# RWKV's low-rank products made for all tokens ahead of the S5 mixer instead of inside each RWKV step

## The chip, the cores and the metric

The kernel runs on one core of a Trainium2 chip. The metric is the time of one execution on the device in microseconds (us). The engines are TensorE (PE for products, PEld for weight loads), VectorE (DVE), ScalarE (ACT), GpSimd (POOL) and SyncE (SP), which here only issues DMAs. L909 means line 909 of the kernel; the lines of the kernel before and of the changed one differ, and the text says which is meant.

## The reference

One layer of a decoder step for 1024 prompt tokens and 8 single sample tokens (1032 columns), model width 1024: half-step SwiGLU FFN, then two token mixers side by side (S5, a diagonal complex state space, and RWKV-7) merged by gates, then a second FFN. What matters here are the three low-rank products of the RWKV branch, two of rank 64 (`rwkv_w2` for the decay, `rwkv_a2` for the key rate) and one of rank 128 (`rwkv_g2` for the output gate), each to 512 channels:

```python
def _wkv7_step(s, inp):                      # one token of the RWKV state, per head
    r, dec, k, v, a, b = inp
    sa = jnp.einsum('bhij,bhj->bhi', s, a)
    s = s * dec[:, :, None, :] + sa[..., None] * b[:, :, None, :] + v[..., None] * k[:, :, None, :]
    return s, jnp.einsum('bhij,bhj->bhi', s, r)

# _rwkv_branch: wd, ad (64 columns each) and gd (128) are parts of the mixed projection
w = -jax.nn.softplus(-(p['rwkv_w0'] + jnp.tanh(wd) @ p['rwkv_w2'])) - 0.5
decay = jnp.exp(-jnp.exp(w))
a = jax.nn.sigmoid(p['rwkv_a0'] + ad @ p['rwkv_a2'])
g = jax.nn.sigmoid(gd) @ p['rwkv_g2']
...
o = (yn + bonus) * g

# _layer
h = h + 0.5 * gt1 * _swiglu(n, p['ffn1_w1'], p['ffn1_w3'], p['ffn1_w2'])
proj = u @ p['w_in']                         # S5 input, RWKV's r k v wd ad gd, two sets of gates
mixed = cur + p['mu_shift'] * (prev - cur)   # token shift
y_s5, ... = _s5_branch(s5_in, ...);  y_rwkv, wkv1 = _rwkv_branch(mixed, ...)
m = jax.nn.sigmoid(gates[..., :D_MODEL]) * y_s5 + jax.nn.sigmoid(gates[..., D_MODEL:]) * y_rwkv
h = h + gt2 * (m @ p['w_out'])               # then a second half-step FFN and a norm
```

All inputs and outputs are fp32.

## The kernel before, in words

Activations lie transposed: 128 channels on the partitions, tokens along the columns, in three chunks of 344 columns (`CH`, slices `cs(c)`). A dense product of fp32 data is made as a split product: weights and activations are each split into a high and a low part of type fp32r (`split`: a cast on ACT, a subtraction on DVE), and high x high (L155), high x low (L156) and low x high (L157) are added in PSUM. The RWKV products inside a step are plain fp32, which PE makes in several passes.

The program's stages, by their time in the profile: FFN 1 (to some 870 us), the input projection, whose RWKV columns are evicted through tiles named "gate" (pool `mp`, four buffers under one tag) and written to DRAM (`sMix`) by SP; the S5 stage (984.9 to 1104.2), which begins with the S5 columns of the projection (`s5_in`, L1427 to L1429) and goes on to `s5_mix`; the RWKV stage (1104.2 to 1548); then the rest of the gate columns, the merge and FFN 2.

In the RWKV stage `rw_run` works through 16 parts of the sequence, each 128 tokens of two of the four channel quarters (`rw_part`). Its loop runs the preparation (`rw_prep`, `rw_solve`) six and four steps ahead of the state chain (`rw_chain`) and of the output (`rw_tail`). In each step `rw_prep` makes the decay and key-rate products of its part (L909: rank 64 padded with zeros to 128 rows, `rw_wa2`) into an "sv" bank and applies the sigmoids on ACT (L912, L914); `rw_tail` makes the gate's product (L1154) and multiplies by it from PSUM (L1155). `rw_sample_vectors` and `rw_sample` do the same for the eight sample tokens, with small products.

Beside the RWKV steps run the gate columns' tiles (`gate_tiles`: L155 to L157, 24 products for each chunk, then a sigmoid eviction to a "gate" tile at L1450, written to DRAM). These are called fillers below: they don't depend on RWKV, and the scheduler puts them into PE's row between the steps' short products. The scheduler sets one order per engine ahead of time, from priorities: a block inside `high_priority(offset=...)` is ordered as though it stood earlier in the program. PSUM banks in the RWKV stage: "mm" 2 (the fillers), "sv" 2, "qd" 2, "ch" 1, "y" 1; in the S5 stage "mm" 4 and "s5" 4. An engine runs its row strictly in order.

Of the kernel before, what the change touches and what calls it, by code (L numbers as in the profile page):

```python
# [65 lines left out]
class Net:  # L66
# [755 lines left out]
    def rw_init(self, rows, keep, tag):  # L822
# [12 lines left out]
        wa2 = self.t(keep, [P, T], "rw_wa2")[:, 0:1024].rearrange("p (z f) -> p z f", z=2)  # L835
        nc.gpsimd.memset(wa2, 0.0)
        nc.sync.dma_start(wa2[0:64, 0, :], i["rwkv_w2"])
        nc.sync.dma_start(wa2[64:128, 1, :], i["rwkv_a2"])
        g2 = self.t(keep, [P, 512], "rw_g2")
        nc.sync.dma_start(g2, i["rwkv_g2"])  # L840
        self.wa2, self.g2w = wa2, g2
# [11 lines left out]
    def rw_lora(self, wad, gd):  # L853

        nc = self.nc
        nc.scalar.activation(wad[0:64, :], wad[0:64, :], AF.Tanh)
        nc.scalar.activation(gd, gd, AF.Sigmoid)
        self.wad, self.sgd = wad, gd
# [35 lines left out]
    def rw_prep(self, n, pool):  # L894
# [11 lines left out]
        pt = self.t(self.pp, [P, 2, 256], "sv")  # L906
        for p, ts in pairs:
            for z in range(2):
                nc.tensor.matmul(pt[:, z, ts], self.wa2[:, z, p * P:(p + 1) * P], self.wad[:, tok], start=True, stop=True)  # L909
        sw, b = new("sw"), new("pb", 2)  # L910
        for p, ts in pairs:
            nc.scalar.activation(sw[:, ts], pt[:, 0, ts], AF.Sigmoid, bias=col("w0", p))  # L912
        for p, ts in pairs:
            nc.scalar.activation(b[:, ts], pt[:, 1, ts], AF.Sigmoid, bias=col("a0", p))  # L914
# [208 lines left out]
    def rw_tail(self, n, py, bon, pool):  # L1123
# [5 lines left out]
        tok, pairs = self.rw_part(n)  # L1129
        s1 = self.t(pool, [P, 4], "t_s1")  # L1130
# [13 lines left out]
        pt, pg = (py[:, z].rearrange("p j t -> p (j t)") for z in (1, 0))  # L1144
# [8 lines left out]
        for p, ts in pairs:  # L1153
            nc.tensor.matmul(pg[:, ts], self.g2w[:, p * P:(p + 1) * P], self.sgd[:, tok], start=True, stop=True)  # L1154
        v.tensor_mul(o, o, pg)  # L1155
# [64 lines left out]
    def rw_sample_vectors(self, pool):  # L1220
# [4 lines left out]
        mx = self.t(pool, [P, 3, 4, NB], "smm")  # L1225
# [4 lines left out]
        for w, dst in enumerate((r, kf, vv)):  # L1230
            for p in range(4):
                nc.sync.dma_start(mx[:, w, p], self.mix_src(p, w, smp))
            v.tensor_copy(dst, mx[:, w].rearrange("p a b -> p b a"))
        yield
        pt = ps([P, 2, 4, NB])
        for p in range(4):
            pc = slice(p * P, (p + 1) * P)
            for z in range(2):
# [540 lines left out]
```

## Time and profile before

| what | value |
|---|---|
| time, median of 3 runs | 2614.97 us (2613.99 to 2616.88) |
| the profiled execution's own time | 2611.84 us |
| its span in the trace | 2610.0 us |
| mean granted PE clock | 0.994 |
| PE busy | 2538.7 us, 97% |
| DVE busy | 1456.4 us, 56% |
| ACT busy | 804.8 us, 31% |
| POOL busy | 330.2 us, 13% |

The shares are averages over stages with different limits; the rows below divide them by stretch. PE's matmuls are pipelined: the duration of one in the trace (0.32 us for 128x344) is longer than the distance between two starts, and the costs below go by starts. A wait is put down to the engine whose signal came last.

### The profile page before, as it was taken

The page shows a single profiled execution, that of the slowest core. Times are in us where ns is not written, and L with a number is a line of the kernel's source. Part 1 is how long each engine was busy: PE and PEld are TensorE (multiplying, and loading weights), DVE is VectorE, ACT ScalarE, POOL GpSimd, SP SyncE. Part 2 cuts the span into 40 slices and gives each one's busy share as a digit, 9 for nine tenths or more (in the row PEclk, how much of TensorE's full clock was granted, in tenths as well). Part 3 has the DMA queues.
Part 4 walks back from the last instruction along what each step waited for, and adds up shares of the span by engine and source line. Part 5 has one row for each costly group of instructions (what it writes and reads, how often), then busy time and mean ns, then how long its engine had stood idle before and what let it go on. Part 6 is the DMA issues. An engine that isn't in the chain of part 4 may idle for free.

```text
span 2610.0 us, 46191 instructions
## 1 busy us (share of the span) xinstructions
PE 2538.7 (97%) x18175; PEld 2390.7 (92%) x18175; DVE 1456.4 (56%) x3716; ACT 804.8 (31%) x1610; POOL 330.2 (13%) x973
## 2 busy tenths in 40 slices
PE   7999999999999999989999999999999999999998
PEld 4899999999999998878877889999999999999997
DVE  5533446555556827687888736476843444444435
ACT  4311111111223422466666543312511111111113
POOL 0000002777100001022232201100000000000001
PEclk9999999999999999999999999999999999999999
DMA  8343332212211414443333337533211111111101
GB/s 273 115 141 116 120 117 75 67 59 72 66 61 46 143 37 132 138 107 78 80 77 83 79 108 229 168 117 103 65 56 42 41 49 49 49 49 49 49 10 66
DMA packets 301677, 233.70 MB, mean 90 GB/s; under 512 B 79954, under 2 KB 265075, under 8 KB 301460
## 3 DMA queue, kind: packets, MB, share of 16 engines
q1 hardware_dynamic: 298642, 224.57, 29.1%
q0 software_dynamic: 1920, 5.27, 0.5%
q8 instruction: 143, 2.34, 0.4%
q10 hardware_dynamic: 898, 0.91, 0.1%
q14 instruction: 74, 0.61, 0.1%
HBM read 186.23 MB, written 44.45 MB: 88 GB/s over the span
## 4 chain that ended last, share of the span: by engine, by line
PE 85%; DVE 8%; issue 2%; ACT 2%; POOL 1%; DMA 1%; SPq 0%; POOLq 0%; DVEq 0%; ACTq 0%
PE mm L155 24%; PE mm L157 24%; PE mm L156 23%; PE ada L217 2%; PE qd L1071 1%; PE sv L982 1%; PE mm L171 1%; PE mm L170 1%; PE mm L169 1%; PE mm L1427 1%; PE mm L1428 1%; PE mm L1429 1%; PE mm L177 1%; PE sv L909 1%; DMA wada<-w_ada 0%
## 5 line engine op out<-in xcount | busy, mean ns | idle before, releaser
L155 PE MATMUL mm<-xa,wh 128*128 128x344 f32 x1944 | 636.0, 328 | 4.6 <-ACT xa L311 3.9
L157 PE MATMUL mm<-xa,wl 128*128 128x344 f32 x1944 | 630.7, 325 | 0.0
L156 PE MATMUL mm<-xb,wh 128*128 128x344 f32 x1776 | 575.2, 324 | 0.3 <-DVE xb L315 0.3
L121 ACT CAST wh<-wr 128x1024 fp32r<-128x1024 f32 x186 | 194.1, 1048 | 724.9 <-PE mm L156 668.2
L339 DVE SCALAR_TENSOR_TENSOR h<-mm,modG,h 128x344 f32<-128x344 f32 (+1 forms) x600 | 338.2, 571 | 131.6 <-PE mm L157 115.1
L156 PE MATMUL mm<-xa,wh 128*128 128x344 f32 x1256 | 402.5, 321 | 1.5 <-DVE xa L122 1.2
L155 PEld LDWEIGHTS mm<-xa,wh 128*128 128x128 f32 x1944 | 367.4, 189 | 32.6 <-issue 16.6
L157 PEld LDWEIGHTS mm<-xa,wl 128*128 128x128 f32 x1944 | 368.2, 189 | 6.0 <-issue 2.5
L122 DVE TENSOR_TENSOR wl<-wr,wh 128x1024 fp32r<-128x1024 f32 x186 | 229.1, 1232 | 226.1 <-ACT wh L121 224.7
L155 PE MATMUL mm<-xb,wh 128*128 128x344 f32 x1088 | 347.8, 320 | 1.4 <-ACT xb L311 1.4
L157 PE MATMUL mm<-xb,wl 128*128 128x344 f32 x1088 | 347.6, 320 | 0.0
L155 PE MATMUL mm<-gh,wh 128*128 128x344 f32 x1056 | 338.7, 322 | 2.4 <-DVE h L339 1.9
L156 PEld LDWEIGHTS mm<-xb,wh 128*128 128x128 f32 x1776 | 335.9, 189 | 4.4 <-issue 1.0
L157 PE MATMUL mm<-gh,wl 128*128 128x344 f32 x1056 | 337.6, 320 | 0.0
L156 PE MATMUL mm<-gl,wh 128*128 128x344 f32 x1056 | 337.4, 320 | 0.0
L361 DVE TENSOR_TENSOR silu<-silu,mm 128x344 f32<-128x344 f32 x132 | 67.6, 512 | 450.7 <-PE mm L157 404.0
L156 PEld LDWEIGHTS mm<-xa,wh 128*128 128x128 f32 x1256 | 236.7, 189 | 2.3 <-DVE xa L122 1.9
L155 PEld LDWEIGHTS mm<-xb,wh 128*128 128x128 f32 x1088 | 204.3, 188 | 2.1 <-ACT xb L311 2.0
L155 PEld LDWEIGHTS mm<-gh,wh 128*128 128x128 f32 x1056 | 198.2, 188 | 8.6 <-DVE h L339 2.8
L157 PEld LDWEIGHTS mm<-xb,wl 128*128 128x128 f32 x1088 | 204.3, 188 | 0.0
L157 PEld LDWEIGHTS mm<-gh,wl 128*128 128x128 f32 x1056 | 198.5, 188 | 0.2
L156 PEld LDWEIGHTS mm<-gl,wh 128*128 128x128 f32 x1056 | 198.5, 188 | 0.1
(528 smaller groups left out, 3268.5 us busy)
## 6 DMA issues: line engine op xcount, KB each, us to landing
wr<-ffn_w SPq DMA_DIRECT2D x132, 512.0 KB
wada<-w_ada SPq DMA_DIRECT2D x144, 256.0 KB
wr<-w_in SPq DMA_DIRECT2D x34, 512.0 KB
sGate<-gate SPq DMA_DIRECT2D x48, 172.0 KB
gate<-sGate SPq DMA_DIRECT2D x48, 172.0 KB
sMix<-gate SPq DMA_DIRECT2D x36, 172.0 KB
sH<-h SPq DMA_DIRECT2D x8, 516.0 KB
h<-sH SPq DMA_DIRECT2D x8, 516.0 KB
```

The costliest lines, as they stand in the source:

```text
L121: nc.scalar.copy(hi, src)
L122: nc.vector.tensor_sub(lo, src, hi.bitcast(F32))
L155: nc.tensor.matmul(pt, wh, xh[:, cols], start=q == 0 and ends[0], stop=False)
L156: nc.tensor.matmul(pt, wh, xl[:, cols], start=False, stop=False)
L157: nc.tensor.matmul(pt, wl, xh[:, cols], start=False, stop=q == last)
L169: nc.tensor.matmul(pt, wh[:, k], xh[k][:, cols], start=k == 0, stop=False)
L170: nc.tensor.matmul(pt, wh[:, k], xl[k][:, cols], start=False, stop=False)
L171: nc.tensor.matmul(pt, wl[:, k], xh[k][:, cols], start=False, stop=k == last)
L177: self.nc.tensor.transpose(out, in_, self.ident[:k, :k])
L217: nc.tensor.matmul(pt[32 * g:32 * g + 32, :], self.cT[:, k, :], wt, start=k == 0, stop=k == KD - 1)
L339: nc.vector.scalar_tensor_tensor(h[d][:, c0:c0 + np_], pt[:, :np_], g[:, d, 0:1], hin[d][:, c0:c0 + np_], op0=ALU.mult, op1=ALU.add)
L361: nc.vector.tensor_mul(s, s, p3)
```

## The change

The three products leave the RWKV steps. In the changed kernel `rw_lora` splits their weights (in one tile, `rw_w`, ranks 64 and 64 on the two halves of the rows and rank 128 in a second block) and, chunk by chunk, the activations `wad` and `gd` into fp32r pairs. A new function `rw_rates`, called after `s5_in` and before `s5_mix`, makes for three chunks and four channel quarters six products on half the rows (L879, decay on the upper and key rate on the lower half, in turn) and three on all rows (L881), each of 344 columns: 108 in all. ACT evicts the three banks, two with a sigmoid (L886) and one with a copy (L888), into "gate" tiles, and SP writes each (L889, 36 DMAs of 172 KB) to new DRAM tensors `sW`, `sA` and `sG`. The RWKV steps read their 128 tokens back: `rw_prep` 64 reads of 64 KB into `sw` (now two buffers) and `pb`, `rw_tail` 32 into `gq`; the sample functions read their columns with 12 small DMAs in place of their small products and sigmoids. Later, a buffer that was called `rw_wa2` is used again as `rw_w`.

```diff
@@ -832,13 +832,11 @@
                    enumerate(("w0", "a0", "kk", "ka", "lnw", "lnb", "rk", "ka1"))}
-        wa2 = self.t(keep, [P, T], "rw_wa2")[:, 0:1024].rearrange("p (z f) -> p z f", z=2)
-        nc.gpsimd.memset(wa2, 0.0)
-        nc.sync.dma_start(wa2[0:64, 0, :], i["rwkv_w2"])
-        nc.sync.dma_start(wa2[64:128, 1, :], i["rwkv_a2"])
-        g2 = self.t(keep, [P, 512], "rw_g2")
-        nc.sync.dma_start(g2, i["rwkv_g2"])
-        self.wa2, self.g2w = wa2, g2
+        wts = self.t(keep, [P, T], "rw_w")[:, 0:1024].rearrange("p (z f) -> p z f", z=2)
+        nc.sync.dma_start(wts[0:64, 0, :], i["rwkv_w2"])
+        nc.sync.dma_start(wts[64:128, 0, :], i["rwkv_a2"])
+        nc.sync.dma_start(wts[:, 1, :], i["rwkv_g2"])
+        self.lw = wts
     def rw_clear(self, pool):
...
@@ -850,12 +848,45 @@
                     nc.sync.dma_start(self.inv_half(x, h), zero)
-    def rw_lora(self, wad, gd):
+    def rw_lora(self, wad, gd, pool):
         nc = self.nc
         nc.scalar.activation(wad[0:64, :], wad[0:64, :], AF.Tanh)
         nc.scalar.activation(gd, gd, AF.Sigmoid)
-        self.wad, self.sgd = wad, gd
+        w = [self.t(pool, [P, 2, 512], f"lw{z}", F32R) for z in range(2)]
+        for z in range(2):
+            self.split(w[0][:, z], w[1][:, z], self.lw[:, z])
+        def part(c):
+            x = [[self.t(pool, [P, CH], f"lx{q}{z}", F32R, bufs=2) for z in range(2)] for q in range(2)]
+            for (hi, lo), src in zip(x, (wad, gd)):
+                self.split(hi, lo, src[:, cs(c)])
+            return x
+        self.lo = w, part
+    def rw_rates(self, pool, offset):
+        nc = self.nc
+        (wh, wl), part = self.lo
+        for c in range(3):
+            (xh, xl), (gh, gl) = part(c)
+            for p in range(4):
+                pc = slice(p * P, (p + 1) * P)
+                pts = [self.t(self.pp, [P, CH], next(self.banks)) for _ in range(3)]
+                for q, (w, x, g) in enumerate(((wh, xh, gh), (wh, xl, gl), (wl, xh, gh))):
+                    for pt, hs in zip(pts, HS):
+                        nc.tensor.matmul(pt, w[hs, 0, pc], x[hs], start=q == 0, stop=q == 2)
+                for q, (w, x, g) in enumerate(((wh, xh, gh), (wh, xl, gl), (wl, xh, gh))):
+                    nc.tensor.matmul(pts[2], w[:, 1, pc], g, start=q == 0, stop=q == 2)
+                with self.tc.high_priority(offset=offset):
+                    for pt, dst, b in zip(pts, (self.sW, self.sA, self.sG), ("w0", "a0", None)):
+                        o = self.t(pool, [P, CH + 1], "gate")[:, 0:CH]
+                        if b:
+                            nc.scalar.activation(o, pt, AF.Sigmoid, bias=self.rv[b][:, p:p + 1])
+                        else:
+                            nc.scalar.copy(o, pt)
+                        nc.sync.dma_start(dst[p][:, cs(c)], o)
     @staticmethod
...
@@ -903,15 +934,11 @@
             nc.sync.dma_start(kf[:, ts], self.mix_src(p, 1, tok))
-        pt = self.t(self.pp, [P, 2, 256], "sv")
+        sw, b = new("sw", 2), new("pb", 2)
         for p, ts in pairs:
-            for z in range(2):
-                nc.tensor.matmul(pt[:, z, ts], self.wa2[:, z, p * P:(p + 1) * P], self.wad[:, tok], start=True, stop=True)
-        sw, b = new("sw"), new("pb", 2)
+            nc.sync.dma_start(sw[:, ts], self.sW[p][:, tok])
         for p, ts in pairs:
-            nc.scalar.activation(sw[:, ts], pt[:, 0, ts], AF.Sigmoid, bias=col("w0", p))
-        for p, ts in pairs:
-            nc.scalar.activation(b[:, ts], pt[:, 1, ts], AF.Sigmoid, bias=col("a0", p))
+            nc.sync.dma_start(b[:, ts], self.sA[p][:, tok])
         Dp = self.t(pool, [P, 4, 65], "Dp", bufs=2)
...
@@ -1127,6 +1154,9 @@
         tok, pairs = self.rw_part(n)
+        g = self.t(pool, [P, 256], "gq")
+        for p, ts in pairs:
+            nc.sync.dma_start(g[:, ts], self.sG[p][:, tok])
         s1 = self.t(pool, [P, 4], "t_s1")
...
@@ -1150,9 +1180,7 @@
         v.tensor_add(o, o, bon)
-        for p, ts in pairs:
-            nc.tensor.matmul(pg[:, ts], self.g2w[:, p * P:(p + 1) * P], self.sgd[:, tok], start=True, stop=True)
-        v.tensor_mul(o, o, pg)
+        v.tensor_mul(o, o, g)
         for p, ts in pairs:
...
@@ -1551,6 +1568,7 @@
         N.sInv = [[N.t(N.dp, [32 * 1040], f"sInv{j}{z}") for z in range(3)] for j in range(4)]
+        N.sW, N.sA, N.sG = ([N.t(N.dp, [P, T], f"s{x}{p}") for p in range(4)] for x in "WAG")
         N.sS = N.t(N.dp, [64, 384], "sS")
...
@@ -1652,9 +1670,10 @@
-                    N.rw_lora(wad, gd)
                     N.rw_init(N.t(mp, [P, CH + 1], "gate")[0:28, 0:P], wl, "mm")
+                    N.rw_lora(wad, gd, N.pool(s5w, "lw"))
                     N.s5_in(xh, xl, X, usT, N.pool(s5w, "s5i"))
+                    N.rw_rates(mp, 30000)
```

PE just after `s5_in`, before: behind the last S5 projection (mm_10079) and a transposition stand the fillers (mm_10920) at once.

```order
L1428 MATMUL mm_10079<-wl_9867,xa_164 128x512
L1429 MATMUL mm_10079<-wh_9866,xb_172 128x512
L177 MATMUL mm_10106<-cf_58,s_us_10104 128x128 x4
L155 MATMUL mm_10920<-xa_157,wh_10915 128x344
L156 MATMUL mm_10920<-xb_165,wh_10915 128x344
```

PE at the same place in the changed kernel; lx are the split activations, lw the split weights, and mm_10139 to mm_10141 the first three banks (decay, key rate, gate).

```order
L1446 MATMUL mm_10098<-wh_9885,xb_184 128x512
L177 MATMUL mm_10125<-cf_58,s_us_10123 128x128 x4
L879 MATMUL mm_10139<-lx_1534_10131,lw_1509_9857 128x344
L879 MATMUL mm_10140<-lx_1534_10131,lw_1509_9857 128x344
L879 MATMUL mm_10139<-lx_1535_10132,lw_1509_9857 128x344
L879 MATMUL mm_10140<-lx_1535_10132,lw_1509_9857 128x344
L879 MATMUL mm_10139<-lx_1534_10131,lw_1510_9858 128x344
L879 MATMUL mm_10140<-lx_1534_10131,lw_1510_9858 128x344
L881 MATMUL mm_10141<-lx_1536_10133,lw_1509_9857 128x344
L881 MATMUL mm_10141<-lx_1537_10134,lw_1509_9857 128x344
L881 MATMUL mm_10141<-lx_1536_10133,lw_1510_9858 128x344
```

The 108 new products stand in one piece between the S5 projection and the next dense tile, with no other product among them; every bank of three has its own eviction and write.

ACT in the middle of the RWKV stage, before: two evictions of fillers (L1450) with eight rows of the steps between them; the widest such distance before is 35 rows.

```order
L1450 ACTIVATE gate_17308<-mm_17283 128x344
L912 ACTIVATE sw_14658<-sv_14653,rw_vec_9835 128x128 x2
L874 ACTIVATE sw_14658<-sw_14658 128x256
L876 ACTIVATE pr_14667<-sw_14658 128x256
L1150 ACTIVATE t_o_14589<-y_14506,rw_vec_9835 128x128 x2
L877 ACTIVATE pt_14666<-pr_14667 128x256
L930 ACTIVATE pt_14685<-kf_14650,rw_vec_9835 128x128 x2
L121 CAST wh_17430<-wr_17429 128x1024
L880 ACTIVATE pt_14666<-pt_14666 128x256
L1450 ACTIVATE gate_17336<-mm_17311 128x344
```

ACT in the changed kernel, the two ends of the place where the evictions (now L1467) stand furthest apart.

```order
L916 ACTIVATE pt_13729<-sw_13721,cf_58 128x256
L1467 ACTIVATE gate_17422<-mm_17397 128x344
L1126 COPY x_2205_13872<-ch_13839 128x128
L916 ACTIVATE pt_13729<-sw_13721,cf_58 128x256
L1130 COPY SUV_13511<-ch_13839 64x2x64
```

```order
L911 ACTIVATE pt_14899<-pt_14899 128x256
L1467 ACT_TABLE_LOAD
L1467 ACTIVATE gate_17450<-mm_17425 128x344
L913 ACTIVATE pt_14899<-pt_14899 128x256
L1467 ACTIVATE gate_17478<-mm_17453 128x344
```

Between gate_17422 and gate_17450 there are 106 rows of RWKV work, among them those of three steps.

PE at the end of the last filler before that place (mm_17453), and where the next one (mm_17487) begins, in the changed kernel.

```order
L156 MATMUL mm_17453<-xb_184,wh_17392 128x344
L157 MATMUL mm_17453<-xa_176,wl_17393 128x344
L1009 MATMUL sv_14278<-R_14261,bk_14265 128x128 x2
L1009 MATMUL sv_14279<-R_14261,bk_14265 128x128 x2
L1009 MATMUL sv_14278<-R_14261,bk_14265 128x128
```

```order
L1129 MATMUL ch_15014<-x_2432_15019,Y_2370_14692 64x64 x4
L959 MATMUL sv_14921<-pt_14918,cf_58 128x256
L1134 MATMUL ch_15014<-SUV_14681,WS_14674 64x64 x4
L155 MATMUL mm_17487<-xa_169,wh_17482 128x344
L156 MATMUL mm_17487<-xb_177,wh_17482 128x344
```

From the one to the other PE's row holds 73 lines (254 products) of RWKV alone; before, the longest such piece is 26 lines (77 products). Counted from one tail's transposition to the next, before has 32 to 66 fillers in each of the 15 distances; the changed kernel has 20, 0 and 3 in three in the middle and 31 to 54 in the others.

## Rows read from the trace of the kernel before

**Rows 1.** The page, parts 1 and 2: span, shares, PE by slice.
```profile
span 2610.0 us, 46191 instructions
PE 2538.7 (97%) x18175; PEld 2390.7 (92%) x18175; DVE 1456.4 (56%) x3716; ACT 804.8 (31%) x1610; POOL 330.2 (13%) x973
...
PE   7999999999999999989999999999999999999998
...
PEclk9999999999999999999999999999999999999999
```
**Rows 2.** The page, part 4: shares of the chain that ended last.
```profile
PE 85%; DVE 8%; issue 2%; ACT 2%; POOL 1%; DMA 1%; SPq 0%; POOLq 0%; DVEq 0%; ACTq 0%
```
**Rows 3.** Busy time by stretch (columns in the first line): dense, S5, RWKV, six steps.
```profile
core 0: us, PE busy (x) PEld busy (x) DVE busy (x) ACT busy (x) POOL busy (x), PEclk, DMA share, GB/s
600.00:840.00 240.00, 240.00 (x1554) 234.44 (x1553) 128.05 (x314) 53.33 (x103) 48.81 (x202) 1.00 0.20 61
984.90:1104.20 119.30, 113.91 (x1061) 105.48 (x1060) 86.94 (x249) 40.96 (x95) 10.89 (x13) 1.00 0.44 132
1104.20:1548.00 443.80, 419.29 (x4577) 356.52 (x4576) 344.82 (x1096) 281.04 (x641) 109.83 (x174) 0.98 0.34 82
1261.30:1396.80 135.50, 129.00 (x1564) 106.70 (x1560) 119.35 (x381) 93.28 (x222) 41.51 (x67) 0.99 0.34 79
```
**Rows 4.** Groups in 1261.3 to 1396.8: line, tiles, count | busy, mean ns | idle before.
```profile
L157 PE MATMUL mm<-xa,wl 128*128 128x344 f32 x81 | 28.2, 348 | 0.0
L155 PE MATMUL mm<-xa,wh 128*128 128x344 f32 x82 | 28.2, 343 | 0.0
L156 PE MATMUL mm<-xb,wh 128*128 128x344 f32 x81 | 27.6, 341 | 0.0
```
**Rows 5.** Timeline of PE around an L909 group: start us, us, instruction.
```profile
1104.22 1.05 PE L909 MATMUL sv<-wad,rw_wa 128*128 128x128 f32 x8
1105.04 0.41 PE L155 MATMUL mm<-xa,wh 128*128 128x344 f32 x1
1105.28 0.32 PE L156 MATMUL mm<-xb,wh 128*128 128x344 f32 x1
1105.44 0.32 PE L157 MATMUL mm<-xa,wl 128*128 128x344 f32 x1
```
**Rows 6.** Timeline of PE around an L1154 group.
```profile
1235.31 0.61 PE L1154 MATMUL y<-gd,rw_g 128*128 128x128 f32 x4
1235.68 0.40 PE L156 MATMUL mm<-xb,wh 128*128 128x344 f32 x1
1235.92 0.32 PE L157 MATMUL mm<-xa,wl 128*128 128x344 f32 x1
```
**Rows 7.** Groups of the whole span: the products removed and a dense tile's eviction.
```profile
L909 PE MATMUL sv<-wad,rw_wa 128*128 128x128 f32 x128 | 19.2, 298 | 3.6 <-DVE W L987 1.9 <-DVE qt L1016 1.6
L1467 ACT ACTIVATE gate<-mm 128x344 f32<-128x344 f32 x24 | 10.9, 458 | 48.3 <-PE mm L157 30.6 <-DVE gate L1472 11.7 <-DVE xa L122 4.1
L1154 PE MATMUL y<-gd,rw_g 128*128 128x128 f32 x64 | 10.3, 284 | 0.0
```
**Rows 8.** Timeline of PE around fp32 products on half the rows (L982).
```profile
1141.14 1.16 PE L982 MATMUL sv<-R,bk 64*128 64x128 f32 x8
1142.23 0.42 PE L157 MATMUL mm<-xa,wl 128*128 128x344 f32 x1
```
**Rows 9.** A 172 KB tile's write: SP's issue, DMA in half-microseconds, landing from POOL's queue.
```profile
990.88 0.32 SPq L1399 DMA_DIRECT2D sMix<-gate  x1
...
990.80:991.30 0.50, 0.50 (x7) 0.41 (x5) 0.24 (x2) 0.00 (x0) 0.00 (x0) 1.00 0.00 0
991.30:991.80 0.50, 0.50 (x7) 0.42 (x6) 0.47 (x4) 0.00 (x0) 0.00 (x0) 1.00 0.14 55
991.80:992.30 0.50, 0.50 (x7) 0.50 (x6) 0.50 (x2) 0.00 (x0) 0.00 (x0) 1.00 0.82 297
...
DMA to landing us min/median/max: 2.3/2.9/5.6
```
**Rows 10.** Busy time and granted clock in two stretches with an idle PE.
```profile
1150.00:1155.00 5.00, 2.78 (x11) 2.74 (x12) 4.92 (x14) 0.00 (x0) 1.36 (x2) 0.74 0.39 92
1125.00:1130.00 5.00, 2.99 (x21) 2.69 (x22) 3.54 (x13) 1.38 (x4) 2.50 (x5) 1.00 0.50 133
```

More of the change, by code (lines that the diff above doesn't have):

```diff
@@ L1143, in rw_tail @@
         v.tensor_mul(y, y, bc(rn))
-        pt, pg = (py[:, z].rearrange("p j t -> p (j t)") for z in (1, 0))
+        pt = py[:, 1].rearrange("p j t -> p (j t)")
         for j in range(4):
@@ L1224, in rw_sample_vectors @@
         sm = self.sm = self.t(pool, [P, 12, NB, 4], "sm")
-        mx = self.t(pool, [P, 3, 4, NB], "smm")
+        mx = self.smx = self.t(pool, [P, 6, 4, NB], "smm")
         nkk, dec, b, kp, r, vv, kf, sw, tmp, e, y, bon = (sm[:, q] for q in range(12))
@@ L1229, in rw_sample_vectors @@
         ps = lambda shape: self.t(self.pp, shape, self.stag)
-        for w, dst in enumerate((r, kf, vv)):
+        for w, dst in enumerate((r, kf, vv, sw, b, None)):
             for p in range(4):
-                nc.sync.dma_start(mx[:, w, p], self.mix_src(p, w, smp))
-            v.tensor_copy(dst, mx[:, w].rearrange("p a b -> p b a"))
+                src = self.mix_src(p, w, smp) if w < 3 else (self.sW, self.sA, self.sG)[w - 3][p][:, smp]
+                nc.sync.dma_start(mx[:, w, p], src)
+            if dst is not None:
+                v.tensor_copy(dst, mx[:, w].rearrange("p a b -> p b a"))
         yield
[L1235 to L1238, printed above, removed]
-                nc.tensor.matmul(pt[:, z, p], self.wa2[:, z, pc], self.wad[:, smp], start=True, stop=True)
-        perm = lambda x: x.rearrange("p a b -> p b a")
-        v.tensor_add(sw, perm(pt[:, 0]), bc("w0"))
-        v.tensor_add(b, perm(pt[:, 1]), bc("a0"))
-        nc.scalar.activation(sw, sw, AF.Sigmoid)
-        nc.scalar.activation(b, b, AF.Sigmoid)
         self.rw_decay(sw, tmp, e, ((-1.0, lambda f, g: v.tensor_mul(dec, f, g)),))
@@ L1344, in rw_sample @@
         v.tensor_add(y, y, bon)
-        pt = ps([P, 4, NB])
-        for p in range(4):
-            nc.tensor.matmul(pt[:, p], self.g2w[:, p * P:(p + 1) * P], self.sgd[:, smp], start=True, stop=True)
         yield
         yt = self.t(pool, [P, 4, NB], "smt", bufs=1)
-        v.tensor_mul(yt, perm(y), pt)
+        v.tensor_mul(yt, perm(y), self.smx[:, 5])
         for p in range(4):
@@ L1730, in hybrid_step @@
                 m3 = N.pool(st, "m3", 5)
-                old = iter(("wad", "gd", "rw_wa2"))
+                old = iter(("wad", "gd", "rw_w"))
                 def mt(d):
```

## The prediction

> **What bounds the kernel now.** I read the page's shares first: TensorE (PE) is busy 2538.7 of 2610.0 us, and its slices are nearly all nines [rows 1]; the chain that ended last is 85% PE and 8% VectorE (DVE) [rows 2]. So a microsecond taken off PE is worth about one, as long as no other engine takes its place. Where that can happen is read by stage. In a dense stretch PE is busy for all of 240.00 us and starts 1554 matmuls: 0.154 us for one 128x344 product of split weights. In the S5 stage, where the new products go, PE is busy 113.91 of 119.30 us. In the RWKV stage it is busy 419.29 of 443.80, and in six of its steps (1261.3 to 1396.8) 129.00 of 135.50 us with DVE at 119.35 and ScalarE (ACT) at 93.28 [rows 3]. There PE is kept busy by products of the gate columns, which fill between the short products of RWKV: 82 + 81 + 81 = 244 of them in the six steps [rows 4], times 0.154 = 37.7 us. Without them a step of 22.6 us holds (129.0 - 37.7) / 6 = 15.2 us of PE work and 119.35 / 6 = 19.9 us of DVE work, about 19.2 without the gate columns' share. **That is the point on which the case turns: RWKV alone is bound by DVE, and PE is only full while fillers stand in its row.**
>
> **Removed: the fp32 products.** One group of L909 (eight passes over 128 columns) starts at 1104.22, and the next product starts 0.82 us later, and that one's successor 0.24 instead of 0.16 later, so 0.90 us in all [rows 5]; 128 records in the trace at 8 each are 16 groups: 14.4 us. L1154 takes 0.37 and the same 0.08 [rows 6]: 0.45, 16 times is 7.2 us. The twelve small products of the sample tokens are put at 1.5 us, between 0.5 and 2.5 (at L909's 0.11 us for a pass they are 1.3, and the wait of what follows for them goes too). Sum: 14.4 + 7.2 + 1.5 = **23.1 us** off PE, all of it in a stage where PE is full. PE also sat idle 3.6 us ahead of L909, released by DVE [rows 7]; the DVE results it waited for are needed by other products soon after, so I count 2 us of it (0 to 3.6).
>
> **Added: 108 fp32r products ahead of the S5 mixer.** Per chunk of 344 columns and per quarter of the channels there are six half-height (K=64) and three full products, 3 x 4 x 9 = 108. At 0.154 to 0.157 us each that is **17.0 us**. Bounds: eight half-height fp32 passes at L982 took 1.09 us against 0.82 for eight full ones at L909 [rows 5, 8], so a half height is not cheaper there; by that ratio the 72 half-height ones would cost 0.19 and the sum is 19. If pairs on the two halves of the rows ran partly beside each other, 0.11 for each, it is 13.4. I take 17.0, the value of the row with the same columns and type.
>
> The Trainium skill (TensorE: Matmul & The Clock Gate, Part 3, packing small matmuls by row and column tiling) says that products that use different halves of the array's rows can run at the same time. By it the 36 x 2 half-height products would save up to 36 x 0.154 = 5.6 us (an estimate from that page). The L982 row, whose passes also alternate between halves, shows no such overlap, so the sum doesn't use it.
>
> **Added: 36 evictions through four buffers, each written out.** The order shows the 108 products in one run, with no other PE work between them. Every three of them need one eviction of ACT (0.458 us at L1467 of the kernel before, the same shape [rows 7]) into a "gate" tile, of which there are four, and the tile is free only when its 172 KB have landed. PE's own pace is 3 x 0.157 = 0.47 us for a tile; ACT's is 0.46, and two more casts for each later chunk bring ACT to some 18.4 us for the stage. The four-buffer ring: one write issued from SP at 990.88 has its data moving from 991.3 on and at most of its rate in 991.8 to 992.3, so it ends some 1.4 us after issue; the same tile written through GpSimd's queue landed after 2.3 us at least, 2.9 in the middle [rows 9]. A buffer's round is then 0.46 + 0.05 + 1.5 to 2.9 = 2.0 to 3.4 us, by four 0.50 to 0.85 us a tile, or 18 to 30.7 us for the 36, against 17.0 of products. The wait is 1 to 14 us. I take **6 us**: the write is on SP's queue, whose row is the nearer, but the 36 writes stand one behind the other and share the DMA engines with others. The SP queue itself issues at 0.32 us a write [rows 9], faster than either.
>
> The Trainium skill (DMA: Bandwidth & Descriptors, Anatomy of one DMA, SWDGE path) gives about 2 us fixed and the bytes at 436 GB/s, so 2.4 us for such a tile (an estimate from that page); the trace's landing times of 2.3 to 2.9 us agree. By that the ring takes 36 x 0.73 = 26 us and the wait would be 9 instead of 6.
>
> **Moved: where the fillers stand.** This is the term I weigh most. The priorities make the gate columns' eviction on ACT stand later than before in one place: in the order shown with the change, ACT has 106 rows between two fillers' evictions in the RWKV stage (line 1467 of the changed kernel, L1450 of the one before), before never more than 35. Only two banks take these products ("mm" in this stage), so PE has nothing to fill with until they are evicted: in PE's row 73 lines of RWKV products stand in a piece (254 products), before at most 26 (77 products). Between successive tails the number of fillers goes from 36 to 53 per step to 20, 0 and 3 in three steps in the middle; some 100 of them move to other places. The filler's own PE time is not lost, but the cover for DVE is. Cost: three steps with 23 fillers hold 3 x (15.2 - 0.90 - 0.45) + 3.5 = 45 us of PE work. DVE needs 3 x 19.2 = 57.6 us, or at the 88% of the time that it is busy in the measured steps, 65. So PE stands idle for 12 to 20 us in these steps, against 6.5 / 6 x 3 = 3.3 us as a rule [rows 3]: 9 to 17 more, and the piece taken by itself (some 33 us of PE work against 53 to 61 of DVE) allows up to 25. Less is possible, since DVE's share includes work for the fillers' neighbours and the chain leads its products by six steps: 5. I take **15**.
>
> **The rest** has one answer each. ACT loses the sigmoids of every step and gains 36 evictions elsewhere; it isn't what PE waits for in the RWKV stage at 93 of 135 us. The 96 reads on SP's queue (64 KB each) are issued a step ahead, and DMA stands at a third of its time there [rows 3]: nothing, or 2 us if a step's first use comes early. Weight and token splits (two of 512 columns, six of 344) lie on ACT and DVE in the S5 stage, where DVE is at 87 and ACT at 41 of 119 us: nothing, or 1.5 for the first one.
>
> **The sum.** Against the profiled execution's 2611.84 us (its span is 2610.0; the median of the runs is 3.1 above it): -23.1 + 17.0 + 6 + 15 - 2 = +13, so 2624.8 profiled and **2628** as a median. What differs by less than 0.2%, 5.2 us, can't be told from no change for this kernel.
>
> **Rivals.**
> A. *Faster: DVE keeps PE supplied anyway.* If the three thin steps need less than some 46 us of DVE, PE is never idle in them and the stretch costs 3; with half-height pairs partly overlapping and a ring at 0.50 us a tile the sum is -23.1 + 13.4 + 2 + 3 - 3.5 = -8, so 2607. For it: PE shares of 95% now with DVE below full; against it: 19.2 us of DVE per step are measured, and the piece has no fillers at all. Chance 0.12.
> B. *About the same: the swap cancels.* Products -23.1 + 17.0, ring 6, stretch 3 to 5, -2: +1 to +3, so 2617. It decides if the steps around the thin ones make up for them, since those have more fillers (DVE can run ahead there by the six steps of lead). Chance 0.20.
> C. *Worse than forecast: the ring at 14 and the stretch at 25*, with products at 17 to 19 and nothing saved in waits: -23.1 + 19 + 14 + 25 = +35, so 2650. The clock can add to it: in 1150 to 1155, with PE busy 2.78 of 5 us, the granted clock was 0.74, though in 1125 to 1130 with 2.99 of 5 it was 1.00 [rows 10]; a PE that stands idle in the long piece may be given less after it. Chance 0.13.
> D. *By the page's rule the halves overlap* and all else is as forecast: 5.6 us less, as 36 half-height products run beside their pair, 2622. The one row that bears on it speaks against it. Chance 0.10.
> The forecast itself, 2621 to 2640: 0.45.
>
> The range leaves out the last of A and of C: 2609 to 2647. Faster by over 0.2%: A, 0.12. Within 0.2%: B, 0.20. Slower: the forecast, C and D, 0.68.
>
> **What would show it.** Right: a stretch of some 40 to 65 us around the middle of the RWKV stage with PE at six or seven tenths, DVE at nine, and PE waiting for DVE and POOL; a stage of 108 products lasting 20 to 27 us with PE waiting for ACT's evictions, and these for the writes of their tiles; the remaining RWKV steps shorter by 1.35 us each. Wrong: PE at nine tenths in the thin steps (A, B), a product stage of 17 us or less (ring, or D, with pairs at one start), or a stage of 30 us and a clock below 0.9 in it (C).

## The result and the profile after

The changed kernel takes **2652.95 us** (median of 4 runs, 2646.76 to 2657.36) against 2614.48 us before: ratio 1.0147, 95% interval 1.0134 to 1.0159, 38 us slower. The sign was forecast, the size was not: 2628 was predicted and the range ended at 2647.

The profiled execution took 2657.36 us; it is the longest of the four, so that the stages below differ by 45.5 us in all and not by 38. Its page, in the parts that answer to [rows 1, 2]:

```profile
span 2655.6 us, 46220 instructions
...
PE 2553.9 (96%) x18067; PEld 2396.2 (90%) x18067; DVE 1451.7 (55%) x3724; ACT 810.8 (31%) x1590; POOL 324.8 (12%) x972
...
PE   7999999999999999988988999999999999999998
...
PEclk9999999999999999999987999999999999999999
...
PE 82%; DVE 8%; ACT 3%; DMA 3%; issue 2%; POOL 1%; SPq 0%; POOLq 0%; ACTq 0%; DVEq 0%
```

PE is busy 15 us longer than before although it has 6 us less of products; its granted clock has a dent in the slices of the RWKV stage, and ACT and DMA have larger shares of the chain (3% each, before 2% and 1%). By stage (the columns are those of [rows 3]; the stages are the projections up to the end of the S5 products, the S5 stage to the last token-shift eviction, the steps up to the first tail, from the first to the last tail, and from there to the last eviction of the S5 output gates). Before:

```profile
600.00:983.70 383.70, 383.46 (x2332) 374.63 (x2330) 201.78 (x501) 106.76 (x197) 53.24 (x214) 1.00 0.22 71
983.70:1158.90 175.20, 160.76 (x1352) 149.85 (x1353) 132.14 (x378) 76.05 (x171) 26.83 (x35) 0.99 0.44 127
1158.90:1233.50 74.60, 68.77 (x601) 60.33 (x599) 58.76 (x183) 49.95 (x113) 19.00 (x29) 0.95 0.32 77
1233.50:1543.30 309.80, 299.30 (x3658) 247.64 (x3659) 239.57 (x782) 192.50 (x449) 74.89 (x123) 0.99 0.34 78
1543.30:1693.00 149.70, 144.60 (x909) 142.07 (x905) 77.75 (x135) 49.58 (x91) 15.75 (x19) 0.98 0.63 198
```

After:

```profile
600.00:985.20 385.20, 384.93 (x2341) 376.12 (x2340) 204.64 (x506) 109.42 (x204) 53.19 (x219) 1.00 0.22 68
985.20:1191.40 206.20, 183.68 (x1429) 165.94 (x1430) 128.75 (x377) 90.72 (x203) 24.43 (x33) 0.94 0.49 145
1191.40:1274.30 82.90, 73.97 (x621) 65.00 (x619) 63.74 (x206) 54.30 (x109) 21.39 (x34) 0.94 0.43 103
1274.30:1578.90 304.60, 277.52 (x3424) 223.30 (x3423) 232.71 (x774) 178.28 (x401) 73.02 (x122) 0.92 0.38 86
1578.90:1738.70 159.80, 152.19 (x937) 149.82 (x933) 75.82 (x126) 48.51 (x87) 14.11 (x18) 0.97 0.63 192
```

The S5 stage grows by 31.0 us for 17 us of new products. From the first to the last tail only 5.2 us are saved, although some 14 us of products left them (eight preparations' 0.90 and fifteen tails' 0.45) and 533 fillers stand there where before had 643. Of the 110 fillers that are missing 50 stand ahead of the first tail (269 where before had 219), in steps that are 8.3 us longer; the others come back in the last stage, 10.1 us longer. PE's idle time between the tails is 304.60 - 277.52 = 27.1 us, before 10.5.

**The thin steps.** The three steps with 20, 0 and 3 fillers:

```profile
1342.00:1363.90 21.90, 15.96 (x195) 11.64 (x191) 21.17 (x79) 14.21 (x33) 6.88 (x10) 0.91 0.43 99
1363.90:1384.10 20.20, 15.61 (x222) 12.37 (x222) 15.40 (x46) 9.67 (x26) 7.09 (x12) 0.75 0.34 74
1384.10:1411.20 27.10, 21.03 (x191) 16.33 (x191) 22.95 (x88) 16.39 (x37) 5.80 (x10) 0.50 0.37 80
```

They last 69.2 us together, no less than three ordinary steps of 22.6, with PE busy 76% of the time and DVE 59.5 us (86%). The granted clock falls over them from 0.91 to 0.50, the lower of its two levels, so that PE counts 52.6 us as busy for what the forecast put at 45 us of work.

**The stage of the new products.** Here the windows are the first part of the piece, the part at low clock, its rest, the dense products behind it, and the time until the S5 mixer begins:

```profile
986.60:994.00 7.40, 6.00 (x38) 4.16 (x37) 1.15 (x3) 5.27 (x12) 0.00 (x0) 1.00 0.53 192
994.00:1001.00 7.00, 7.00 (x27) 4.96 (x27) 0.15 (x2) 4.92 (x11) 0.00 (x0) 0.54 0.70 252
1001.00:1009.70 8.70, 8.55 (x47) 5.93 (x46) 0.01 (x1) 6.70 (x14) 0.00 (x0) 0.98 0.71 250
1009.70:1013.40 3.70, 3.70 (x22) 3.43 (x22) 0.16 (x2) 1.07 (x3) 0.00 (x0) 1.00 0.68 201
1013.40:1017.40 4.00, 0.01 (x1) 0.00 (x0) 0.00 (x0) 0.43 (x1) 0.00 (x0) 1.00 1.03 364
1017.40:1021.40 4.00, 3.96 (x17) 3.53 (x17) 2.08 (x10) 0.45 (x1) 0.00 (x0) 0.63 0.66 239
```

The 108 products last 23.1 us, as forecast (17 + 6), 7 of them at low clock. What was not forecast stands behind them: PE waits 4.0 us, the clock falls, and DVE, which before is busy with the S5 mixer from 990 on, has next to nothing to do for 33 us. The timeline tells why (start us, us, engine; a q behind the engine's name is its DMA queue):

```profile
1009.20 0.36 ACTq L772 DMA_DIRECT2D s_dbc<-s_d  x1
1009.63 0.40 SPq L666 DMA_DIRECT2D q_bp<-s_bp  x1
1009.69 0.17 DVE L790 COPY s_us<-s_usT 128x32 f32<-128x32 f32 x1 [15.54 <-issue]
...
1010.23 0.35 ACTq L776 DMA_DIRECT2D s_hr<-state_s_re  x1
...
1017.43 0.33 PE L177 MATMUL s<-cf,s_hr 128*128 128x128 f32 x1 [4.02 <-DMA s_hr<-state_s_re]
```

The mixer's states are loaded from ACT's queue and its tables from SP's. Each engine issues in the order of its row, and in the changed kernel these loads stand behind all but the last evictions and writes of the new products. In the kernel before the first load of the states went out ahead of the end of the S5 projection (983.7), and the product on it did not wait (rows between the two left out):

```profile
978.64 0.38 ACTq L776 DMA_DIRECT2D s_hr<-state_s_re  x1
988.35 0.27 PE L177 MATMUL s<-cf,s_hr 128*128 128x128 f32 x1
```

A second thing may hold the mixer here. Its tiles take the memory of the split weights and activations (the expectation of e4 says so), and DVE's copy at L790, whose input was there from 986.9 on, starts at 1009.69, just as the last of the new products ends. That the memory is what it waited for is inferred from these times. For the loads, e7 tells the two reasons apart.

### The profile page after: what moved, and what is told of

Read it like the earlier page. It is cut to its first block, busy times and chain, and to the rows that moved or that the text cites. A ratio compares the mean times of both kernels' runs of the same rounds, so it can differ in the third digit from the quotient of the medians.

```text
span 2655.6 us, 46220 instructions
## 1 busy us (share of the span) xinstructions
PE 2553.9 (96%) x18067; PEld 2396.2 (90%) x18067; DVE 1451.7 (55%) x3724; ACT 810.8 (31%) x1590; POOL 324.8 (12%) x972
## 4 chain that ended last, share of the span: by engine, by line
PE 82%; DVE 8%; ACT 3%; DMA 3%; issue 2%; POOL 1%; SPq 0%; POOLq 0%; ACTq 0%; DVEq 0%
PE mm L155 23%; PE mm L156 23%; PE mm L157 23%; PE ada L217 2%; PE qd L1098 1%; PE mm L171 1%; PE mm L170 1%; PE mm L169 1%; PE mm L1444 1%; PE mm L1445 1%; PE mm L1446 1%; PE mm L177 1%; PE sv L1009 1%; DMA wr<-w_out 0%; POOL bk L992 0%
```

## The experiments

Two places can hold the 25 us beyond the forecast: the steps without fillers, and the stage of the new products with what stands behind it. They were tried by repairing one thing at a time. Runs of before on the same chips had medians of 2615.4 to 2616.3 us.

**e1_evict.** The sigmoid eviction of a gate column's tile gets the high priority that its weight load has.

```diff
-                nc.scalar.activation(g, pt, AF.Sigmoid)
+                with self.tc.high_priority(offset=woff):
+                    nc.scalar.activation(g, pt, AF.Sigmoid)
```

> The changed kernel, with one block added: the sigmoid eviction of a gate column's tile is put in a high-priority block, like its weight load. That closes the piece of 73 rows without fillers in TensorE's row (longest piece 254 products before, 67 now); the rest of the program is the same. Theory 1 (the RWKV steps without fillers cost idle TensorE time of 17 us and some 15 us at the low clock behind it): 2653 - 32 = 2621 us, between 2612 and 2632. Rival (VectorE bounds the steps whether or not fillers stand in them, and the loss lies in the S5 stage): 2645 to 2655 us.

Measured: 2631.06 us (ratio 1.0065, 1.005 to 1.008), 22 us less than the changed kernel. The steps without fillers cost what theory 1 says, at the smaller end of the saving expected (2612 to 2632).

**e2_ring7.** Seven buffers in place of four.

```diff
+        ring = cycle([pool, pool2])     # pool2: three more "gate" tiles
...
-                        o = self.t(pool, [P, CH + 1], "gate")[:, 0:CH]
+                        o = self.t(next(ring), [P, CH + 1], "gate")[:, 0:CH]
...
```

> The changed kernel, the 36 evictions of the new products going by turns into the four gate buffers and three more of their own (seven in place of four); order of every engine unchanged. Theory 1 (the ring of four buffers costs 6 us and the granted clock near it some more): 2653 - 6 to 10 = 2643 to 2647 us, and the stage of 108 products takes 18 us in place of 23. Rival (the products on half the rows or the clock set the pace, not the buffers): 2650 to 2654 us, the stage still 22 to 24 us.

Measured: 2653.82 us, no gain, a miss: 2643 to 2647 had been expected. The stage did shrink, from 23.1 to 17.8 us, with PE never waiting in it (busy time of that window):

```profile
984.10:1001.90 17.80, 17.80 (x110) 12.79 (x110) 1.23 (x3) 15.87 (x36) 0.00 (x0) 1.00 0.86 298
```

The mixer's first product on its states (timeline of PE) still waits for their load:

```profile
1012.26 0.33 PE L177 MATMUL s<-cf,s_hr 128*128 128x128 f32 x1 [2.29 <-DMA s_hr<-state_s_re]
```

So the ring cost the stage 5.3 us, of which 2.6 are left at the last token-shift eviction (the S5 stage takes 203.6 us in place of 206.2), and none is seen in the time; the runs of the two kernels spread over 4 and 11 us, so a gain of a few us can't be ruled out. The edit also changed the order, against what was expected: the states' load stands behind all 36 evictions and a token-shift eviction (L1405 at 1005.75) and goes out at 1007.42, so this run is not the ring alone. The 36 writes are 36 x 172 KB, some 6.3 MB; at the 298 GB/s that DMA moved here they alone would take 21 us, and the mixer's tables stand behind them and four small reads on the same queue (q_bp issued at 1007.45). That the loads are what kept the gain is tried in e11.

**e3_removal.** The products left out; constants are written once and read by the steps.

```diff
-                    N.rw_lora(wad, gd, N.pool(s5w, "lw"))
+                    N.rw_fill(mp)            # 0.5 from one tile into sW, sA, sG
...
-                    N.rw_rates(mp, 30000)
```

> The changed kernel without its 108 new products, their activation splits and evictions: the 36 DRAM pieces are filled from one tile with the constant 0.5 ahead of the S5 projection, and the RWKV steps read them as before, so decay, key rate and gate are constants. TensorE's row has no long piece without fillers in it (15 fillers in the thinnest step). Theory 1 (removal is worth its 23 us of products, since TensorE is full elsewhere): 2614.5 - 23 + 3 = 2594 us, between 2588 and 2602. Rival (VectorE bounds the steps, so products taken out of them give little): 2606 to 2616 us.

Measured: 2613.06 us (ratio 0.9992, 0.9982 to 1.0002): taking out 23 us of products gave nothing. This is the rival's number, and theory 1's 2594 fell in this form. Between its tails stand 653 fillers, with 15 in the thinnest step, and PE is idle 22 us there:

```profile
1236.60:1547.80 311.20, 289.05 (x3544) 235.37 (x3543) 237.21 (x779) 184.03 (x409) 73.60 (x122) 0.96 0.39 91
```

Whether the steps can't be shorter or only lacked fillers is told by e9.

**e4_early.** The call moved ahead of the S5 projection.

```diff
+                    N.rw_rates(mp, 30000)
                     N.s5_in(xh, xl, X, usT, N.pool(s5w, "s5i"))
-                    N.rw_rates(mp, 30000)
```

> The changed kernel, with the call that makes the 108 products moved from behind the S5 projection to ahead of it. The S5 mixer's tiles take the memory of the split weights and activations, so behind the projection the mixer waits for the last eviction; ahead of it the projection's products stand between. TensorE's row also has no long piece without fillers (74 products). Theory 1 (starved piece 32 us, and of the stage's loss the part that lies between the products' end and the mixer's start, some 8 us, goes too): 2653 - 40 = 2613 us, between 2604 and 2624. Rival (the stage of the new products costs the same wherever it stands, and the RWKV steps don't gain from fillers): 2640 to 2655 us.

Measured: 2651.01 us, a miss: 2613 had been expected, and this is the rival's number, although the order of the RWKV stage is that of e3. Against e3 the 108 products cost 38 us here. In the trace PE waits 4.3 us among the first of them for the cast of the gate's activations, and the clock is at its lower level for 30 us, though PE is busy for 27 of them (busy time of that stretch, and of the part of it in which PE never waits):

```profile
937.50:967.50 30.00, 27.02 (x99) 18.28 (x99) 1.98 (x4) 17.93 (x38) 0.00 (x0) 0.50 0.56 196
949.60:967.60 18.00, 18.00 (x69) 12.48 (x69) 0.08 (x1) 11.25 (x24) 0.00 (x0) 0.50 0.62 220
```

At that level nine products take 2.3 us in place of 1.3 (e12's timeline, in the last section).

**e5_before_evict** and **e6_removal_evict.** The block of e1 in the kernel before (a control), and in that of e3, where it happens to open a piece of 208 products without fillers.

> Control for the first experiment: the kernel before with the same high-priority block around the gate columns' eviction. Its TensorE row has no long piece without fillers either way (77 products before, 69 now). Theory 1 (the block helps the changed kernel only by closing the piece): 2610 to 2618 us. Rival (the block itself speeds up the evictions, so the 22 us of the first experiment are no cost of the piece): 2590 to 2600 us.

> The kernel of the third experiment (the products are left out, constants are read) with the high-priority block of the first. Here the block does not close a piece but opens one: two steps without fillers, a piece of 208 products in place of 74. Theory 1 (pieces without fillers cost idle TensorE time and low clock, whatever made them): 2613 + 10 to 20 = 2623 to 2633 us. Rival (the block helps by itself, or fillers don't matter): 2595 to 2614 us.

Measured: 2616.16 us (ratio 1.0001, 0.9991 to 1.0010) and 2622.22 us (1.0023, 1.0012 to 1.0033; 9 us above e3, 1 us below the range expected). The same edit gains 22 us, nothing, or loses 9 us, according to whether it closes, finds none, or opens such a piece. So it is the piece that costs.

**e7_mix.** The 108 products dealt out among those of the S5 projection.

```diff
         for s in range(8):
             pt = proj(slice(s, NP, 8))
+            next(rates)                 # rw_rates as a generator, nine products a turn
+            if s % 2:
+                next(rates)
...
```

> The changed kernel with the 108 products dealt out among the S5 projection's (nine of the new ones after each of the eight projections, eighteen after every second), so that dense products stand between two of their evictions. The RWKV stage's order is that of the run with the early call (no long piece, thinnest step 15 fillers). Theory 1 (the stage of the new products costs 40 us in place of 17 because TensorE waits for evictions and its clock falls to half behind the waits): 2651 - 20 = 2631 us, between 2626 and 2638. Rival (the products cost that by themselves, by their shape): 2645 to 2652 us.

Measured: 2637.58 us, 13 us under e4 with the same RWKV order. The clock is 1.00 throughout the projection and PE is never idle there; what is left is a wait of 3.5 us for the states' load, as in the changed kernel (rows between these left out):

```profile
1003.01 0.23 ACT L914 ACTIVATE sm<-sm 128x32 f32<-128x32 f32 x1 [0.30 <-DVE sm L913]
1003.69 0.35 ACTq L776 DMA_DIRECT2D s_hr<-state_s_re  x1
1009.88 0.47 PE L177 MATMUL s<-cf,s_hr 128*128 128x128 f32 x1 [3.46 <-DMA s_hr<-state_s_re]
```

The last of the new products ends at 996.0 here and the last write goes out at 997.5, and still the load waits until 1003.69: in ACT's row it stands behind the sample tokens' decay (L914), whose inputs are read back from what was written. In this run it is the order of the row that holds the load, and not the memory of the new products' operands.

**e8_full.** The 72 half-height products made on all rows.

```diff
-                    for pt, hs in zip(pts, HS):
-                        nc.tensor.matmul(pt, w[hs, 0, pc], x[hs], start=q == 0, stop=q == 2)
+                    for pt, z in zip(pts, (0, 2)):   # weights padded with zeros
+                        nc.tensor.matmul(pt, w[:, z, pc], x, start=q == 0, stop=q == 2)
...
```

> The changed kernel with the 72 half-height products made on all 128 rows, against weights padded with zeros, as the kernel before had them; order otherwise the same. Theory 1 (half-height pairs run side by side, and TensorE's row is too thin there, so the clock falls; full ones cost 0.157 us each and hold the clock): the stage 20 to 24 us, the time 2648 to 2655 us, with the granted clock at 1.00 in the stage. Rival (no pairs, the clock falls because of the waits for evictions): same stage time or longer by up to 6 us, clock still 0.5 in part of it, 2653 to 2660 us.

Measured: 2652.97 us, the same; the stage 22.4 us at a clock of 1.00. The shape of the products doesn't matter for the time here. Nor is it the clock that makes this stage long: e8's is hardly shorter at full clock, and e13's, the same products as in the changed kernel, takes 22.3 us with the clock at 1.00:

```profile
985.30:1007.60 22.30, 20.37 (x109) 14.39 (x108) 1.30 (x4) 16.67 (x35) 0.00 (x0) 1.00 0.67 239
```

**e9_removal_even** and **e10_before_even.** A priority for the gate evictions ahead of the RWKV steps' work, so that the fillers are dealt out evenly; in e3's kernel and, as a control, in the kernel before.

```diff
-                nc.scalar.activation(g, pt, AF.Sigmoid)
+                with self.tc.high_priority(offset=woff and woff + 5000):
+                    nc.scalar.activation(g, pt, AF.Sigmoid)
```

> The kernel of the third experiment (products left out, constants read) with the gate columns' evictions at a still higher priority, ahead of the RWKV steps' work, which deals the fillers out evenly: at least 36 between two tails (15 before), the longest piece without one 67 products. Theory 1 (products taken out of the steps are worth their time, but only where TensorE's row has fillers for the time that they leave): 2614 - 18 to 22 = 2592 to 2597 us. Rival (the steps' own chain of VectorE, ScalarE and TensorE sets their length, and the removal gives nothing in any order): 2606 to 2616 us.

> Control: the kernel before with the same priority as in the run with evenly dealt fillers. Its row goes from 32 to 66 fillers between tails to 36 to 56. Theory 1 (it has no thin step to mend): 2610 to 2618 us. Rival (the priority is worth something by itself): 2595 to 2606 us.

Measured: 2590.18 us (ratio 0.9896, 0.9881 to 0.9911; 2 us below the range expected) and 2615.71 us (0.9996, 0.9985 to 1.0008). The removal is worth 25 us, all of what was forecast for it (23.1 + 2), once the steps hold enough fillers: 807 between the tails in place of 653, in 319 us in place of 311, with PE idle 9.8 us. In the kernel before there was nothing to mend. Between e9's tails:

```profile
1235.60:1554.80 319.20, 309.42 (x3698) 256.39 (x3699) 239.59 (x794) 189.14 (x421) 71.11 (x122) 0.99 0.41 98
```

**e11_mix2** and **e12_mix2_even.** The products among the first six S5 projections only, so that the evictions end some 15 us before the mixer is due; and the same with e9's priority.

```diff
-            next(rates)
-            if s % 2:
-                next(rates)
+            if s < 6:
+                next(rates)
+                next(rates)
```

> The run with the products dealt out among the S5 projection's, now eighteen after each of the first six projections in place of all eight, so that the last eviction and write lie some 15 us before the projection's end. The S5 mixer's loads (its states on ScalarE's queue, its tables on SyncE's) stand behind these evictions and writes. Theory 1 (the late loads cost TensorE 5 us of waiting after the projection, and some low clock): 2637.6 - 6 = 2629 to 2634 us. Rival (the mixer starts late for another reason, the wait stays): 2636 to 2641 us.

> Both repairs in one kernel that computes all: the 108 products after the first six S5 projections, the fillers dealt out evenly. Theory 1: the removal's 18 to 22 us less, the products' 17 and some 2 for splits more: 2612 to 2618 us, about the kernel before. Rival (each repair was an accident of one order): 2628 to 2640 us.

Measured: 2627.82 us, 10 us under e7 and 1 us below the range expected, with no wait for the states' load left; and **2606.65 us** (ratio 0.9958, 0.9941 to 0.9974), 9 us under the kernel before while it computes everything, and 5 us below the range expected. Its stages:

```profile
600.00:1001.40 401.40, 401.12 (x2445) 387.05 (x2443) 206.95 (x517) 128.24 (x247) 52.96 (x218) 1.00 0.26 84
1001.40:1171.50 170.10, 156.43 (x1313) 146.34 (x1314) 124.72 (x359) 70.23 (x154) 21.15 (x29) 0.98 0.46 133
1171.50:1251.00 79.50, 70.88 (x627) 62.44 (x625) 66.21 (x205) 53.70 (x112) 26.95 (x37) 1.00 0.45 108
1251.00:1570.20 319.20, 309.04 (x3698) 256.40 (x3699) 239.26 (x796) 189.14 (x421) 71.29 (x122) 0.99 0.41 97
1570.20:1688.20 118.00, 107.08 (x662) 103.82 (x659) 70.88 (x113) 37.97 (x67) 13.64 (x18) 0.97 0.72 220
```

The stage with the products is 17.7 us longer than before; the S5 stage is 5.1 us shorter, the steps up to the first tail take 4.9 us longer, with 269 fillers in place of 219; the last stage is 31.7 us shorter, since more of the gate columns were made between the tails, which take 9.4 us longer for it.

**e13_even.** e9's priority in the changed kernel, the products left in their own place.

> The changed kernel with the evenly dealt fillers of the twelfth run (at least 34 between two tails), the 108 products left in one piece behind the S5 projection. Theory 1 (the piece costs its waits, its half clock and the S5 mixer's late loads, the thin steps the rest): 2607 + 20 to 25 = 2627 to 2632 us, so that the thin steps were worth 21 to 26 us of the change's loss. Rival (the early place matters only through the order that comes with it): 2606 to 2616 us.

Measured: 2628.08 us (ratio 1.0055, 1.0038 to 1.0071), in the range expected, and it divides the loss:

| from | to | us | what it is |
|---|---|---|---|
| before 2615.4 | e9 2590.2 | -25.2 | removal, fillers even |
| e9 2590.2 | e12 2606.7 | +16.5 | the 108 products, among dense ones |
| e12 2606.7 | e13 2628.1 | +21.4 | the products in one piece ahead of the mixer |
| e13 2628.1 | changed 2653.0 | +24.9 | the steps without fillers |

Not all of the 21.4 us is the place of the products. e13's S5 stage is 35.5 us longer than e12's and begins 17.5 us earlier, so that 18.0 us arise up to the last token-shift eviction; the other 3 come later, where the steps hold 743 fillers and not 807. The S5 stage of e13:

```profile
983.90:1189.50 205.60, 183.13 (x1429) 166.03 (x1430) 128.47 (x377) 90.53 (x202) 24.65 (x33) 0.95 0.49 146
```

## Why the prediction was wrong

- **Removed, -23.1 and -2 for vanished waits:** right in size, with a condition that the forecast did not state for it: measured -25.2 with even fillers (e9 against before), -2.5 with the fillers as they fell in e3.
- **Added, +17.0:** right. Measured 16.5 (e12 against e9). The value was right and the reason only partly, as the last section tells.
- **The ring of four buffers, +6: the first step that failed.** The stage took 23 us as forecast, and with seven buffers 5.3 less. (That the 6 came so near is partly luck: it was picked between 1 and 14, and in the half-microseconds of [rows 9] DMA also carried five loads that SP issued from 991.26 on.) But the term stopped at the end of the products. Not asked was which other instructions stand behind the evictions on ACT and behind the writes on SP; they are the loads of the S5 mixer, and the forecast had looked at SP's queue for its issue time alone. Against e12 the one piece cost 21.4 us. Of the excess of 15 over the ring, 3 are e13's fewer fillers, and e7 and e11 show 10 for late loads with the products already spread out. Whether it is as much in the piece, and what the low clock, the mixer's memory and a mixer that runs late share in it, was not separated.
- **The steps without fillers, +15 with bounds 5 to 25: the second term mis-sized.** Measured 24.9 (e13), and 22 in e1. The mechanism was right, to the three steps, and the working nearly so: 45 us of PE work, 57.6 to 65 us of DVE. The steps took 69.2 us, above the upper of these, with DVE busy for 59.5 of them; that PE's half clock lengthened the products in the chain between is likely and was not shown by itself. By the forecast's own working this is 69.2 - 45 - 3.3 = 20.9 us (3.3 is what PE idles in three steps as a rule). The choice of 15, below the middle of the 9 to 25 worked out, leaned on the lead of six steps, which did not shorten these; nothing in the trace had shown PE without fillers.
- **The rest, put at nothing:** not tried by itself, but e9 and e12, which have the reads in them, come out at -25.2 and -8.7 where the forecast's terms give -25.1 and -8.1.
- **The rivals:** C, with the ring at 14 and the stretch at 25, gave 2650, the nearest to the result; it got 0.13, and the range cut it off at 2647. Its stretch came true and the fall of the clock too, but not its ring of 14 (5.3) nor its products of 19 (16.5); the late loads, which it did not name, stand in for them, so its nearness is partly luck. (By the ratio that the prediction names, 1.09 to 0.82, a half-height product would be 0.205 us and the products 20, not 0.19 and 19.) A's condition, that PE would never be idle in the thin steps, is refuted by their windows. B's, that other steps make up for them, is refuted by e1 and e13. D is half right: see the last section.
- **What was to be seen:** of the three marks for the forecast two were there (PE at 76% with DVE at 86%, for 69 us in place of 40 to 65; products lasting 20 to 27 us), and the third, the remaining steps shorter by 1.35 us each, was not: from tail to tail the other twelve last 234.6 us, and the same twelve before 242.0, 0.6 us each. Of C's mark, a stage of 30 us with a clock below 0.9, the clock was there (0.54 in 994 to 1001) and the length was not. The time between the first and the last tail lies between 304 and 321 us in all of these kernels, whatever was taken out; what differs is how many fillers fit into it: 643 before, 533 after, 743 in e13, 807 in e9 and e12. At 0.154 us each, the 210 fillers between the changed kernel and e13 are 32 us of work done beside the steps, less 6.4 us by which the steps grew: 26, against 24.9 measured.

## What to carry to other kernels

Where one engine is kept full by fillers, products taken out of its steps are worth something only if more fillers move in; count fillers per step in the order of the changed kernel, and price a step without them at its full length less what PE does in it. Where a batch of work with evictions and writes is put in front of a stage, look for that stage's loads on the same queues, and let the batch end early enough, among dense products, that the loads go out in time. One reordering that an edit brings along can outweigh the edit: an order with and an order without the thin steps differed by 22 to 25 us here for the same work (e1, e3 against e9, e13).

## What the runs showed of the hardware that was not expected

Half-height fp32r products on the two halves of the rows do run partly side by side, against what the fp32 row [rows 8] suggested. The timeline of PE at full clock, in e12 (the end of one group is the start of the next):

```profile
946.24 0.74 PE L879 MATMUL mm<-lx,lw 64*128 64x344 f32 x6
946.91 0.73 PE L881 MATMUL mm<-lx,lw 128*128 128x344 f32 x3
947.58 0.82 PE L879 MATMUL mm<-lx,lw 64*128 64x344 f32 x6
```

And in e8, with products on all rows:

```profile
985.81 1.19 PE L884 MATMUL mm<-lx,lw 128*128 128x344 f32 x6
986.84 0.63 PE L886 MATMUL mm<-lx,lw 128*128 128x344 f32 x3
987.31 1.24 PE L884 MATMUL mm<-lx,lw 128*128 128x344 f32 x6
```

Six half-height products take 0.67 us (0.112 each) against 1.03 us for six full ones (0.172 each). The three full products behind the half-height ones, though, take 0.67 us (0.223 each) against 0.47 us (0.157 each) behind full ones: nine take 1.34 in place of 1.50 us, at most 2 us in all instead of the 5.6 of rival D. The Trainium skill (TensorE: Matmul & The Clock Gate, Part 3, packing small matmuls by row and column tiling) says that products on different rows of the array run at the same time; these rows agree for the pairs, and the dearer full-height products behind them are not in its model. Why those are dearer was not tried.

The granted clock, once it had fallen to 0.50 around a wait of 4.3 us in e4, stayed there for 30 us of which PE was busy 27, the last 18 of them without a wait; in the changed kernel it was back after 7 us of the same products (994 to 1001). With dense products between (e7, e12) it didn't fall in the projection at all.
